# Holding the last activation blocks of a layer on TensorE's queue until the gate products or the prompt's keys are done

## The chip, the cores and the metric

The kernel runs on one core of one Trainium2 chip. The metric is the time of one execution on the device in microseconds. A core has five engines that each work through a queue of their own: TensorE (PE in the profile, its weight loads PEld), VectorE (DVE), ScalarE (ACT), GpSimd (POOL) and SyncE (SP), which here issues the transfers between main memory and the core's own memory. Engines wait for each other only through semaphores.

## The reference, cut to what matters

One step of a two-layer backbone over two streams: a prompt of 128 tokens and a sample of 512 tokens, 1024 wide. Each layer is a mixer (layer 0: retention and a short convolution; layer 1: a gated delta rule and a convolution module) and then an expert mixer in which every token picks 16 of 16,384 experts for each of 8 heads:

```python
def peer_ffn(h, wq, keys, u_tab, v_tab):
    q = (x @ wq).reshape(T, H_P, 2, D_KEY // 2)
    s = jnp.einsum('thpd,hpnd->thpn', q, keys)
    s1, i1 = lax.top_k(s[:, :, 0], TOPK)
    s2, i2 = lax.top_k(s[:, :, 1], TOPK)
    ...
    top_s, sel = lax.top_k(cand_s, TOPK)
    eidx = jnp.take_along_axis(cand_i, sel, axis=-1)
    gates = jax.nn.softmax(top_s)
    ...
        act = jax.nn.gelu(jnp.einsum('td,tkd->tk', xt, u_tab[et]))
        return jnp.einsum('tk,tkd->td', gt * act, v_tab[et])
```

Each layer ends in `xp + ga2p * peer_ffn(hp, ...)` and `xs + ga2s * peer_ffn(hs, ...)`, and layer 1 starts from what layer 0 gives.

## The kernel before, in words

Of the sample's four tiles of 128 tokens, three (384 tokens) are computed densely: all 16,384 experts are multiplied with all tokens, and a matrix of gates, zero for experts that were not picked, selects afterwards. The fourth tile and the prompt gather the rows that they picked (GpSimd issues the gathers, VectorE multiplies and sums the rows). Experts are taken as 128 rows `e` of 128 experts.

`peer_dense` (L1405 on) does the dense part of a layer in two stages.

The first stage has a background: the generator `acts` (L1381) computes for each row `e` a block of activations. A block loads 512 KB of `u` (`ur<-ut`), splits it into a high and a low part (`uh`, a cast on ScalarE; `ul`, a subtraction on VectorE), and runs 24 matmuls of 128x384 (`A<-hHL,uh` and `A<-hHL,ul`, in `peer_act`, L1368); ScalarE applies gelu (`w<-A`, L1379) and the queue of SyncE stores the result to main memory (`wd<-w`). The matmuls of the foreground call `tick` (L165), and a rate decides how many blocks the background has traced by then. The foreground is, in layer 0, the choice of experts and the gates of the sample, and then `mid()` = `odd_p`: the prompt's mixer of layer 1 and the prompt's choice of experts (`peer_start`). In that, 16 pieces of `wq` are projected (`pt<-hT,w`), four times the products with the keys follow (`sc<-keys,q`), `top_keys` (L1160) picks the best on VectorE, and `peer_topk` (lines 1197 to 1238, `top`, `both`, `tv`, `sel`, `eq`, `ef`) finishes the choice there. In layer 1 there is no `mid()`, and the foreground at the stage's end is `gate_matrix` (L1309): three tiles of 8 blocks with 4 groups each, a group being four matmuls `G<-o,o` from one-hot matrices `o` made by VectorE (L1335, L1346) and ScalarE (L1343, L1344). A block of gates is copied (`gst<-G`) and stored (`gd<-gst`).

In the second stage a row `e` loads 512 KB of `v` (`vr<-v`, L1427), its gates (`gt<-gd`, L1433) and its activations (`w<-wd`, L1438). ScalarE casts `vh`, VectorE makes `vl`, multiplies `w<-w,gt` (L1516), ScalarE casts `wh`, VectorE makes `wl`, and 36 matmuls of 128x512 add to `dacc`. Some rows ("fused") have their activation block in this stage. Meanwhile VectorE sums the gathered rows (`row<-row,hn`, `gacc<-row,gel,gacc`, L1274 and L1284).

Each engine runs its instructions in one fixed order. It is set when the kernel is built, by a scheduler that simulates the engines; within `manual_schedule` blocks the named engines keep the order of the code (GpSimd in the first stage, GpSimd, VectorE and ScalarE in the second). `self.mark` is the last gelu: a gather that is issued outside the prompt's lane waits for it (L1248).

Of the kernel before, what the change touches and what calls it, by code (L numbers as in the profile page):

```python
# [2 lines left out]

# [14 lines left out]
P = 128  # L18
# [7 lines left out]
TB = 16  # L26
# [32 lines left out]
SP = (P0, P1)  # L59
MT = 2.4  # L60
GDN_W = 4
PARTS = ((0, 16), (16, 24), (24, 40), (40, 48))
NFIRST = 20

# [19 lines left out]
class Kern:  # L84
    def __init__(self, ctx, tc, A):
        self.tc, self.nc, self.A = tc, tc.nc, A
        e = ctx.enter_context
        self.cp = e(tc.tile_pool(name="consts", bufs=1))
        self.xpool = e(tc.tile_pool(name="x", bufs=1))
        self.rowp = e(tc.tile_pool(name="rowp", bufs=6))  # L90
        self.hpool = e(tc.tile_pool(name="hn", bufs=1))
        self.sm = e(tc.tile_pool(name="sm", bufs=2))
        self.n = 0
        self.bg, self.in_bg = None, False
        self.mods = {}
        self.lane = ""
        self.queue = tc.nc.sync
        self.wt = lambda name: self.pt("w", name)
        self.more, self.turn = None, 0
        self.steps_per_act = self.side_per_act = self.side_rate = self.side_owed = 0.0  # L100
        self.mark = None
        self.side = None

    def nm(self, s):
# [54 lines left out]

    def mm(self, out, lhsT, rhs, start, stop):  # L160

        self.nc.tensor.matmul(out, lhsT, rhs, start=start, stop=stop)  # L162
        self.tick(rhs.free_size() / 600.0)

    def tick(self, us):  # L165

# [933 lines left out]
    def peer_prep(self, st, l, begin=None):  # L1100
# [24 lines left out]
        for jg in range(4):  # L1125
            kt = self.wt("keys")[:, :512]
            self.queue.dma_start(kt, A["keys"][l, jg])
            qs = []
            for j in range(4 * jg, 4 * jg + 4):
                if not late:  # L1130
                    parts(j)
                b = self.proj_split(st, *ws.pop(j)) if st.s else self.proj_t(st, hT, ws.pop(j))
                q = self.a2(st, "q")
                nc.scalar.copy(q[:, :st.T], b[:, :st.T])
                qs.append(q)
                if late:
                    parts(j + 2)
                if pend:
                    self.top_keys(*pend.pop(0))
            for it in range(st.nt):  # L1140
                b = self.bank("sc")
                for j in range(4):
                    self.mm(b[:, j * P:(j + 1) * P], qs[j][:, it * P:(it + 1) * P],
                                     kt[:, j * P:(j + 1) * P], start=True, stop=True)
                t = self.vt("s")
                nc.scalar.copy(t, b)
                if jg == 0:
                    top = (st.scp.tile([P, 512], F32, tag="top", bufs=4, name=self.nm("top")) if st.s
                           else self.vt("top"))
                    st.top[it] = top.rearrange("p (v h c k) -> p v h c k", v=2, h=8, c=2)  # L1150
                pend.append((st, it, jg, t))
                if len(pend) > late:
                    self.top_keys(*pend.pop(0))
# [152 lines left out]
            V.tensor_tensor(acc[half], acc[half], g[half], op=OP.mult)  # L1306
            V.tensor_tensor(st.x[it][:, sl], st.x[it][:, sl], acc[half], op=OP.add)

    def gate_matrix(self, st, tiles, gd):  # L1309

        nc = self.nc
        V, S, PE = nc.vector, nc.scalar, nc.tensor
        for n, it in enumerate(tiles):
            cols = self.gp.tile([P, 4, P], F32, tag="gcols", bufs=1, name=self.nm("gcols"))
            for j in range(2):
# [7 lines left out]
                b = self.bank("gT", (P, P))  # L1323
                self.transpose_to(b, fi)
                V.tensor_copy(cols[:, j, :], b)
            b = self.bank("gT", (P, P))
# [3 lines left out]
            for tb in range(P // TB):  # L1330
                out = self.gp.tile([P, P, TB], F32, tag="gst", bufs=3, name=self.nm("gst"))
                for q in range(TB // 4):
# [4 lines left out]
                    b = self.bank("G", (P, 4, P))  # L1337
                    for j in range(4):
                        t = tb * TB + q * 4 + j
                        o1 = self.gp.tile([P, P], F32, tag="o1", bufs=16, name=self.nm("o1"))  # L1340
                        if j == 3:

                            S.activation(o1, self.iota128, AF.Square, bias=cols[:, 3, t:t + 1])  # L1343
                            S.activation(o1, o1, AF.Relu, scale=-1.0, bias=cols[:, 2, t:t + 1])  # L1344
                        else:
                            V.tensor_scalar(o1, self.iota128, cols[:, 0, t:t + 1], cols[:, 2, t:t + 1],  # L1346
                                            op0=OP.is_equal, op1=OP.mult)
                        self.mm(b[:, j, :], o2[:, j, :], o1, start=True, stop=True)
                    S.copy(out[:, :, q * 4:q * 4 + 4], b.rearrange("p t i -> p i t"))
                nc.sync.dma_start(gd[:, :, n * (P // TB) + tb].rearrange("g p q t -> p g q t"),  # L1350
                                  out.rearrange("p (g q) t -> p g q t", q=GQ))

# [15 lines left out]
    def peer_act(self, st, u, w):  # L1368
# [9 lines left out]
            self.mm(a[:, :N], ul[:, cs], hH[c], start=False, stop=(c == KC - 1))  # L1378
        return self.nc.scalar.activation(w, a[:, :N], AF.Gelu_apprx_tanh)  # L1379

    def acts(self, st, l, es, up, wd, steps):  # L1381

        ur = {i: self.u_load(l, es[i], up) for i in range(2)}
# [2 lines left out]
        for i, e in enumerate(es):  # L1386
# [1 line left out]
                ur[i + 2] = self.u_load(l, es[i + 2], up)  # L1388
            un = self.u_split(i + 1, ur.pop(i + 1), up) if i + 1 < len(es) else None
            w = up.tile([P, wd.shape[2]], F32, tag="w", name=self.nm("w"))  # L1390
            self.mark = self.peer_act(st, u, w)
            self.nc.sync.dma_start(wd[e], w)
            u = un
            due += self.steps_per_act if st.nt - 1 in st.gate else 0
# [10 lines left out]
    def peer_dense(self, st, l, mid=None):  # L1405
# [40 lines left out]
        with self.banks(5), self.tc.tile_pool(name=self.nm("up"), bufs=2, reuse_waits="tile") as up:  # L1446
# [27 lines left out]
            self.rate = RG if mid else RH  # L1474
            self.steps_per_act = STEPS[l]["gates"]
            with self.tc.tile_pool(name=self.nm("gp"), bufs=2, reuse_waits="tile") as self.gp:
                self.gate_matrix(st, tiles, gd)
            if mid:
                for _ in self.side or ():
                    pass  # L1480
# [304 lines left out]
```

## Time and profile before

| | us |
|---|---|
| median of three timed runs | 4157.77 (4157.51 to 4159.66) |
| the profiled execution | 4148.63 |
| its span in the trace | 4146.9 |
| TensorE busy | 3808.5 (92%) |
| VectorE busy | 3393.6 (82%) |
| ScalarE busy | 1510.3 (36%) |

A row of the timeline gives the start in us, the duration in us, the engine, the line, the operation with what it writes and reads, how many instructions it groups, and in brackets how long the engine had idled before it and what ended that. The profile records each of these matmuls twice, so a group of four `G` matmuls is "x8" there, and some records are left out.

### The profile page before, as it was taken

To read this page: it belongs to the slowest core of one execution; us is meant where nothing else is said; L and a number is where in the kernel's file an instruction comes from. 1 tells how busy PE (TensorE), PEld (TensorE's weight loads), DVE (VectorE), ACT (ScalarE), POOL (GpSimd) and SP (SyncE) were. 2 spreads that over 40 slices of the span, in tenths; PEclk is the share of its full clock that TensorE was granted. 3 is DMA by queue.
4 is the path that set the end of the run, shared out by engine and by line. 5 is a ranking of instruction groups with operands and counts; after the bars stand their busy time and mean duration, and the time that the engine had idled before them with its cause. 6 is when DMAs were issued, how large, how long until landed. Compare 5 with 4: busy or idle time off the path is not lost. (4 is left out here: it accounts for less than half of the span.)

```text
span 4146.9 us, 56434 instructions
## 1 busy us (share of the span) xinstructions
PE 3808.5 (92%) x19406; PEld 3124.2 (75%) x19406; DVE 3393.6 (82%) x7171; ACT 1510.3 (36%) x2810; POOL 1457.4 (35%) x1080
## 2 busy tenths in 40 slices
PE   6789879899999998999998998889989989999997
PEld 4453549866899996788884457859989978888886
DVE  5568799997699976988887999569888977788887
ACT  2110123232664542333332364533335733333333
POOL 0106563450024441444435764033011034444442
PEclk9899589999999999999999999899999999999999
DMA  8549698897699888999978977167367899999995
GB/s 291 189 135 358 211 343 292 300 350 251 195 316 361 329 314 301 323 365 359 352 278 328 340 240 250 42 205 278 113 203 234 258 324 325 323 332 333 346 337 186
DMA packets 445776, 1161.99 MB, mean 280 GB/s; under 512 B 39728, under 2 KB 190640, under 8 KB 445232
## 3 DMA queue, kind: packets, MB, share of 16 engines
q1 hardware_dynamic: 290800, 595.23, 40.6%
q0 software_dynamic: 154688, 563.15, 38.4%
q8 instruction: 152, 2.49, 0.2%
q14 instruction: 136, 1.11, 0.1%
HBM read 1062.48 MB, written 95.75 MB: 279 GB/s over the span
## 5 line engine op out<-in xcount | busy, mean ns | idle before, releaser
L1246 POOL DMA_INDIRECT row<-u,eid x512 | 676.7, 1322 | 1318.1 <-ACT w L1379 683.2
L1246 POOL DMA_INDIRECT row<-v,eid x512 | 751.1, 1467 | 1084.4 <-DVE gacc L1284 629.8
L162 PE MATMUL A<-hHL,uh 128*128 128x384 f32 x4096 | 1085.0, 344 | 14.6 <-ACT uh L1355 11.3
L162 PEld LDWEIGHTS A<-hHL,uh 128*128 128x128 f32 x4096 | 748.6, 191 | 46.6 <-issue 20.3
L162 PE MATMUL A<-hHL,ul 128*128 128x384 f32 x2048 | 705.3, 345 | 44.7 <-DVE ul L1356 44.6
L1274 DVE SCALAR_TENSOR_TENSOR row<-row,hn 128x1024 f32<-128x1024 f32 x512 | 614.1, 1218 | 102.0 <-DMA row<-u,eid 91.8
L1284 DVE SCALAR_TENSOR_TENSOR gacc<-row,gel,gacc 128x1024 f32<-128x1024 f32 x508 | 649.8, 1279 | 26.8 <-DMA row<-v,eid 22.1
L162 PE MATMUL dacc<-vh,wh 128*128 128x512 f32 x1536 | 483.5, 396 | 50.2 <-ACT wh L1355 50.2
L162 PE MATMUL dacc<-vl,wh 128*128 128x512 f32 x1536 | 477.9, 392 | 0.0
L162 PE MATMUL pt<-hT,w 128*128 128x128 f32 (+1 forms) x2176 | 455.6, 366 | 23.2 <-DMA w<-wq 12.1
L162 PEld LDWEIGHTS A<-hHL,ul 128*128 128x128 f32 x2048 | 391.4, 191 | 67.5 <-DVE ul L1356 51.0
L162 PEld LDWEIGHTS pt<-hT,w 128*128 128x128 f32 x2176 | 305.2, 196 | 166.7 <-issue 139.8
L1355 ACT CAST uh<-ur 128x1024 fp32r<-128x1024 f32 x256 | 268.1, 1048 | 442.4 <-PE A L162 330.5
L1356 DVE TENSOR_TENSOR ul<-ur,uh 128x1024 fp32r<-128x1024 f32 x256 | 311.7, 1218 | 102.2 <-ACT uh L1355 93.4
L162 PE MATMUL dacc<-vh,wl 128*128 128x512 f32 x1536 | 391.9, 389 | 0.0
L1355 ACT CAST wh<-w 128x384 fp32r<-128x384 f32 (+1 forms) x235 | 137.5, 585 | 659.8 <-DVE w L1516 457.2
L162 PEld LDWEIGHTS dacc<-vh,wh 128*128 128x128 f32 x1536 | 283.4, 189 | 123.8 <-ACT wh L1355 72.6
L1356 DVE TENSOR_TENSOR vl<-vr,vh 128x1024 fp32r<-128x1024 f32 x256 | 312.7, 1221 | 64.8 <-ACT vh L1355 58.2
L162 PEld LDWEIGHTS dacc<-vl,wh 128*128 128x128 f32 x1536 | 291.0, 189 | 62.7
L162 PEld LDWEIGHTS dacc<-vh,wl 128*128 128x128 f32 x1536 | 288.6, 188 | 60.1
L1355 ACT CAST vh<-vr 128x1024 fp32r<-128x1024 f32 x256 | 267.6, 1045 | 54.0 <-PE dacc L162 45.5
L1356 DVE TENSOR_TENSOR wl<-w,wh 128x384 fp32r<-128x384 f32 (+1 forms) x235 | 152.2, 648 | 127.6 <-ACT wh L1355 127.6
(373 smaller groups left out, 5000.3 us busy)
## 6 DMA issues: line engine op xcount, KB each, us to landing
ur<-ut SPq DMA_DIRECT2D x256, 512.0 KB
vr<-v SPq DMA_DIRECT2D x256, 512.0 KB
gd<-gst SPq DMA_DIRECT2D x48, 1024.0 KB
gt<-gd SPq DMA_DIRECT2D x96, 512.0 KB
wd<-w SPq DMA_DIRECT2D x203, 192.0 KB
w<-wd SPq DMA_DIRECT2D x203, 192.0 KB
w<-wq SPq DMA_DIRECT2D x48, 512.0 KB
w<-ada_m SPq DMA_DIRECT2D x48, 512.0 KB
```

Of the source, the lines that this page charges most:

```text
L162: self.nc.tensor.matmul(out, lhsT, rhs, start=start, stop=stop)
L1246: f = self.nc.gpsimd.indirect_dma_start(out=t, out_offset=None, in_=table, in_offset=bass.IndirectOffsetOnAxis(ap=idx, axis=0))
L1274: V.scalar_tensor_tensor(u, u, 1.0, hn, op0=OP.mult, op1=OP.mult, accum_out=act[:, k:k + 1])
L1284: V.scalar_tensor_tensor(gacc, v, t[:, k:k + 1], gacc, op0=OP.mult, op1=OP.add)
L1355: self.nc.scalar.copy(hi, src)
L1356: self.nc.vector.tensor_tensor(lo, src, hi.bitcast(F32), op=OP.subtract)
```

## The change

A table `HOLD` names, for each layer, two marks with a number of blocks: blocks with fewer than that many after them are to come behind the mark. For layer 0 the marks are the prompt's keys, the second product group (`("p", 1, 1)`, 5 blocks) and the last (`("p", 1, 3)`, 3 blocks); for layer 1 the gate blocks 19 (8 blocks) and 23, the last (4 blocks). The products with the keys and the gate products note their last matmul in `self.marks`. Before it issues a held block, `acts` yields until the foreground has traced the mark, and `issue_after` then puts the block's instructions on TensorE behind the mark's on that queue, without a semaphore.

```diff
+HOLD = (((("p", 1, 3), 3), (("p", 1, 1), 5)), ((("G", 1, 23), 4), (("G", 1, 19), 8)))
...
+        self.marks = {}
...
-        self.nc.tensor.matmul(out, lhsT, rhs, start=start, stop=stop)
+        f = self.nc.tensor.matmul(out, lhsT, rhs, start=start, stop=stop)
         self.tick(rhs.free_size() / 600.0)
+        return f
...
+                self.marks[st.name, l, jg] = f.ins
...
+                self.marks["G", l, n * (P // TB) + tb] = f.ins
...
+    def held(self, l, left):
+
+        return next((key for key, n in HOLD[l] if left < n), None)
+
     def acts(self, st, l, es, up, wd, steps):
...
-            self.mark = self.peer_act(st, u, w)
+            key = self.held(l, len(es) - 1 - i)
+            while key and key not in self.marks:
+                yield
+            with self.tc.issue_after(self.marks[key]) if key else nullcontext():
+                self.mark = self.peer_act(st, u, w)
             self.nc.sync.dma_start(wd[e], w)
```

In the built kernel, layer 0 has five held blocks (numbers 123 to 127 of its 128): two stand behind the second products with the keys and three behind the last. Layer 1 has eight: its blocks 67 to 74 of 75, four behind gate block 19 and four behind the last gate product. Lines below the change move by 1 to 13.

On TensorE in layer 0, after the last two products with the keys (`sc`), there stood only products that spread the modulation (`bc`) and then the second stage's `dacc`. Before:

```order
L162 MATMUL sc_13248<-keys_13194,q_13233 128x128
L162 MATMUL sc_13248<-keys_13194,q_13246 128x128
L162 MATMUL bc_13376<-bc_d_13383,ones 128x128
L162 MATMUL bc_13376<-bc_d_13386,ones 128x128
L162 MATMUL bc_13390<-bc_d_13391,ones 128x128
L162 MATMUL bc_13390<-bc_d_13394,ones 128x128
L162 MATMUL bc_13390<-bc_d_13397,ones 128x128
L162 MATMUL bc_13390<-bc_d_13400,ones 128x128
L162 MATMUL dacc_13449<-vh_13455,wh_13460 128x512
```

And now, from the same two products on:

```order
L164 MATMUL sc_13136<-keys_13082,q_13121 128x128
L164 MATMUL sc_13136<-keys_13082,q_13134 128x128
L164 MATMUL A_13232<-hHL_2802,uh_12976 128x384
L164 MATMUL A_13232<-hHL_2810,uh_12976 128x384
L164 MATMUL A_13232<-hHL_2802,ul_12977 128x384
L164 MATMUL A_13232<-hHL_2803,uh_12976 128x384
L164 MATMUL A_13232<-hHL_2811,uh_12976 128x384
```

Three whole blocks, 72 matmuls, now stand between the last key product and the second stage, with the `bc` among and behind them.

On VectorE in layer 0 the choice of the prompt's experts (`sel`, `both`, `eq`, `ef`) is queued together with the second stage's first row (`vl`, `w`, `wl`). Before, the first `vl` stood in the middle of the first search:

```order
L1212 MAX_INDEX sel_13296<-tv_13295,both_13282 128x8 x2
L1211 MAX tv_13295<-both_13282 128x8
L1213 MATCH_REPLACE both_13282<-tv_13295,both_13282 128x50 x2
L1356 TENSOR_TENSOR vl_13456<-vr_13408,vh_13455 128x1024
L1212 MAX_INDEX sel_13296<-tv_13295,both_13282 128x8
L1516 TENSOR_TENSOR w_13414<-w_13414,gt_13410 128x384
L1213 MATCH_REPLACE both_13282<-tv_13295,both_13282 128x50
```

Now, the same `vl` (`vl_13456`) among the last comparisons:

```order
L1228 TENSOR_TENSOR eq_13348<-eq_13348,both_13170 128x800
L282 TENSOR_SCALAR bc_d_21593<-cst,mod_5430 128x128
L1229 TENSOR_REDUCE ef_13227<-eq_13348 128x2x8
L1226 TENSOR_TENSOR eq_13352<-sf_13225,iota_96 128x800
L1361 TENSOR_TENSOR vl_13456<-vr_13408,vh_13455 128x1024
L1529 TENSOR_TENSOR w_13414<-w_13414,gt_13410 128x384
L1228 TENSOR_TENSOR eq_13352<-eq_13352,both_13170 128x800
L1361 TENSOR_TENSOR wl_13461<-w_13414,wh_13460 128x384
```

The first `vl` has moved behind the whole search (`tv`, `sel`) and 10 of the 18 `eq` and `ef` operations; the other eight come between the rows that follow.

On ScalarE in layer 1 the gate copies (`gst<-G`) were followed at once by the second stage's first cast `vh`. Before:

```order
L1344 ACTIVATE o_6175_27956<-o_6175_27956,gcols_27320 128x128
L1349 COPY gst_27892<-G_27895 128x128x4
L1349 COPY gst_27892<-G_27912 128x128x4
L1349 COPY gst_27892<-G_27929 128x128x4
L1349 COPY gst_27892<-G_27946 128x128x4
L1355 CAST vh_28010<-vr_27966 128x1024
```

And now, with `w<-A` the gelu of a held block:

```order
L1353 COPY gst_27721<-G_27775 128x128x4
L1360 CAST uh_27888<-ur_27852 128x1024
L1384 ACTIVATE w_27858<-A_27859 128x384
L1384 ACTIVATE w_27892<-A_27893 128x384
L1360 CAST uh_27923<-ur_27886 128x1024
L1384 ACTIVATE w_27927<-A_27928 128x384
L1384 ACTIVATE w_27955<-A_27956 128x384
L1360 CAST vh_28010<-vr_27832 128x1024
```

The first `vh` now stands behind the gelus of the last held blocks, the very last one included.

## Rows read from the trace of the kernel before

**Rows 1.** Windows: stretch; its length; PE, PEld, DVE, ACT, POOL busy; PEclk; DMA; GB/s.

```profile
1554.30:1591.00 36.70, 36.70 (x174) 29.10 (x173) 23.71 (x41) 11.44 (x24) 13.96 (x14) 1.00 0.89 334
...
1639.70:1652.60 12.90, 2.14 (x13) 1.41 (x11) 12.47 (x84) 3.15 (x6) 0.00 (x0) 0.74 1.00 387
1652.60:1712.70 60.10, 53.96 (x216) 40.98 (x217) 58.85 (x106) 19.36 (x27) 28.42 (x12) 0.97 0.87 305
...
3231.50:3294.00 62.50, 62.17 (x462) 61.85 (x462) 59.88 (x163) 49.53 (x120) 4.30 (x4) 1.00 0.84 250
3294.00:3330.30 36.30, 31.59 (x225) 26.75 (x223) 35.07 (x102) 32.73 (x82) 2.12 (x2) 1.00 0.88 266
```

**Rows 2.** Timeline of PE, from the prompt's projections to the second stage of layer 0.

```profile
1599.65 1.49 PE L162 MATMUL pt<-hT,w 128*128 128x128 f32 x6
...
1619.64 2.05 PE L162 MATMUL pt<-hT,w 128*128 128x128 f32 x16 [0.59 <-DMA w<-wq]
1622.77 5.62 PE L162 MATMUL pt<-hT,w 128*128 128x128 f32 x48 [1.08 <-DMA w<-wq]
...
1639.12 0.61 PE L162 MATMUL sc<-keys,q 128*128 128x128 f32 x4
...
1652.62 1.22 PE L162 MATMUL dacc<-vh,wh 128*128 128x512 f32 x2 [9.88 <-ACT wh L1355]
...
1659.04 0.73 PE L162 MATMUL dacc<-vh,wh 128*128 128x512 f32 x2 [0.43 <-ACT wh L1355]
```

**Rows 3.** Timeline of PE, the thirteenth and fourteenth expert row of that stage.

```profile
1712.76 0.61 PE L162 MATMUL dacc<-vh,wh 128*128 128x512 f32 x2
...
1716.84 0.61 PE L162 MATMUL dacc<-vh,wh 128*128 128x512 f32 x2
```

**Rows 4.** Timeline of DVE, the prompt's choice of experts and the second stage's first rows.

```profile
1640.42 0.86 DVE L1165 MAX8 top<-s 128x8 f32<-128x128 f32 x4
...
1645.61 0.29 DVE L1197 CAST top<-top 128x256 f32<-128x256 uint32 x1
...
1650.15 1.22 DVE L1356 TENSOR_TENSOR vl<-vr,vh 128x1024 fp32r<-128x1024 f32 x1
...
1659.77 1.28 DVE L1284 SCALAR_TENSOR_TENSOR gacc<-row,gel,gacc 128x1024 f32<-128x1024 f32 x1
1660.97 0.82 DVE L1222 TENSOR_TENSOR eq<-sf,iota 128x640 f32<-128x640 f32 x1
...
1675.64 0.99 DVE L1222 TENSOR_TENSOR eq<-sf,iota 128x800 f32<-128x800 f32 x1
```

**Rows 5.** Timeline of PE in layer 1, from the last activations to the second stage.

```profile
3287.22 0.51 PE L162 MATMUL A<-hHL,uh 128*128 128x384 f32 x2
...
3287.74 0.51 PE L162 MATMUL A<-hHL,uh 128*128 128x384 f32 x2
...
3290.16 3.73 PE L162 MATMUL G<-o,o 128*128 128x128 f32 x32
3293.65 0.42 PE L162 MATMUL A<-hHL,ul 128*128 128x384 f32 x1
...
3327.75 1.16 PE L162 MATMUL G<-o,o 128*128 128x128 f32 x8 [0.21 <-DVE o L1335]
3329.12 1.16 PE L162 MATMUL G<-o,o 128*128 128x128 f32 x8 [0.21 <-DVE o L1335]
3343.99 1.22 PE L162 MATMUL dacc<-vh,wh 128*128 128x512 f32 x2 [13.71 <-ACT wh L1355]
```

**Rows 6.** ACT and DVE, a gelu and layer 1's first row of the second stage.

```profile
1588.83 0.49 ACT L1379 ACTIVATE w<-A 128x384 f32<-128x384 f32 x1 [4.53 <-PE A L162]
...
3338.30 1.04 ACT L1355 CAST vh<-vr 128x1024 fp32r<-128x1024 f32 x1 [7.40 <-DMA vr<-v]
...
3342.79 0.56 DVE L1516 TENSOR_TENSOR w<-w,gt 128x384 f32<-128x384 f32 x1 [2.18 <-DMA w<-wd]
```

**Rows 7.** Waits of PE from 3344 to 4122 us: waited in total, times, longest.

```profile
PE dacc L162 <- ACT wh L1355: 34.2, 20, 13.7
```

More of the change, by code (lines that the diff above doesn't have):

```diff
@@ L1 @@
-from contextlib import ExitStack, contextmanager
+from contextlib import ExitStack, contextmanager, nullcontext
 from itertools import chain, islice
@@ L1142, in peer_prep @@
                 for j in range(4):
-                    self.mm(b[:, j * P:(j + 1) * P], qs[j][:, it * P:(it + 1) * P],
+                    f = self.mm(b[:, j * P:(j + 1) * P], qs[j][:, it * P:(it + 1) * P],
                                      kt[:, j * P:(j + 1) * P], start=True, stop=True)
+                self.marks[st.name, l, jg] = f.ins
                 t = self.vt("s")
@@ L1307, in add_out, with gate_matrix @@
             V.tensor_tensor(st.x[it][:, sl], st.x[it][:, sl], acc[half], op=OP.add)
-    def gate_matrix(self, st, tiles, gd):
+    def gate_matrix(self, st, l, tiles, gd):
         nc = self.nc
@@ L1347, in gate_matrix @@
                                             op0=OP.is_equal, op1=OP.mult)
-                        self.mm(b[:, j, :], o2[:, j, :], o1, start=True, stop=True)
+                        f = self.mm(b[:, j, :], o2[:, j, :], o1, start=True, stop=True)
                     S.copy(out[:, :, q * 4:q * 4 + 4], b.rearrange("p t i -> p i t"))
+                self.marks["G", l, n * (P // TB) + tb] = f.ins
                 nc.sync.dma_start(gd[:, :, n * (P // TB) + tb].rearrange("g p q t -> p g q t"),
@@ L1476, in peer_dense @@
             with self.tc.tile_pool(name=self.nm("gp"), bufs=2, reuse_waits="tile") as self.gp:
-                self.gate_matrix(st, tiles, gd)
+                self.gate_matrix(st, l, tiles, gd)
             if mid:
```

## The prediction

> **What bounds the kernel now.** I read the windows first, stretch by stretch, because the 92% of TensorE's busy time is an average. Then came TensorE's timeline at the two places where the held blocks go, VectorE's timeline there, and last what TensorE waits for afterwards.
>
> In layer 0 three stretches follow each other. From 1554.3 to 1591 TensorE has no idle time at all: five activation blocks (123 to 127) and the last projection of the prompt's mixer share it, and VectorE is busy 23.71 of 36.7 us [rows 1]. Then come the prompt's projections from 1599.65, with short waits for pieces of `wq` (0.59 and 1.08 us behind the second keys), and the last key product, which starts at 1639.12 and ends about 1639.7 [rows 2]. Call that end T. From T to the second stage's first `dacc` (1652.62) TensorE stands for 9.88 us, and VectorE is busy 12.47 of 12.9 us [rows 1, 2]. From there to 1712.7 VectorE is busy 58.85 of 60.1 us, so it sets the pace: twelve expert rows take 1712.76 - 1652.62 = 60.14 us, 5.01 each, and the next one takes 4.08 us, which is TensorE's own time for a row [rows 1 to 3]. VectorE is the bound here because the prompt's choice of experts and the dense rows share it.
>
> In layer 1, from 3231.5 to 3294, TensorE (62.17 of 62.5 us) and VectorE (59.88) are both full; then only gate products are left, and TensorE follows VectorE's one-hot matrices (35.07 of 36.3 us busy) with a group every 3329.12 - 3327.75 = 1.37 us [rows 1, 5]. The last gate product ends near 3330.3, and the first `dacc` starts at 3343.99 after 13.71 us of idle time, which is a chain of loads and the splits of the first row [rows 5, 6].
>
> **The change in layer 0.** The five blocks leave the stretch before the prompt's projections. A block is 24 matmuls, and three take 3287.74 - 3287.22 = 0.52 us, so a block is 8 x 0.52 = 4.16 us and five are 20.8 us [rows 5]. The projections start earlier by at most that. What remains of TensorE's work there is 36.7 - 20.8 = 15.9 us, but VectorE keeps 23.71 us less four subtractions `ul` of about 1.2 us, 18.9 us [rows 1, 4], in front of the prompt's last sum, and each step through it (spread, copy, sum) is a round trip that the blocks hid. The stretch cannot be shorter than 18.9 us, which makes 17.8 us the most that the start can move with VectorE in its present order. If TensorE falls to half of its clock while it waits, its 15.9 us become about 32, and the start moves only some 5 us. Between 5 and 17.8 us I take 10, a little nearer to the slow end, because round trips add to VectorE's work.
>
> Two of the blocks (8.3 us) come back among the projections, behind the second keys. There they fill the waits of 0.59 and 1.08 us [rows 2]. T moves by -10 + 8.3 - 1.7 = -3.4 us; with the ends above, by +1.6 to -11.
>
> Behind T stand the other three blocks, 12.5 us on TensorE, beside VectorE's work. They cover the 9.88 us of idle time, and at most 2.6 us stand beyond. The price is the order on VectorE. Before, the first `vl` started 9.73 us after the search's first `MAX8` (1640.42 to 1650.15) [rows 4]. Now it stands behind the whole search and 10 of 18 comparisons. Operations in a row start 0.08 us before the recorded end of the one ahead (1659.77 + 1.28 against 1660.97), so 0.08 is taken off each duration. Worked out from T: 0.7 us to the first `MAX8`; 5.2 us to the cast at 1645.61; 15.4 us from there to the first `eq` (1660.97), less two rows' dense work that stood in it (twice `vl` 1.14, `w` 0.48, `wl` the same, `gacc` 1.2, 6.6 us), 8.8 us; six 640-wide comparisons of 0.74, 4.4 us; four 800-wide of 0.91, 3.6 us; one held `ul`, as large as a `vl`, 1.1 us; and twelve small `bc_d`, by the nearest row of a small tile (the cast's 0.29 us) some 0.2 us each, 2.5 us [rows 4, 6]. That is 26.3 us to `vl`, and 1.2 us for `vl` and 1.2 us from `w` to `dacc` (3342.79 to 3343.99) follow [rows 4 to 6]: 29 us from T, where 12.9 stood before. The three blocks end 12.5 us after T, so about 16 us of idle time follow them.
>
> Some of it comes back, since the search is nearly over by then. Eight comparisons remain, two to a row, so four rows go at 5.01 us and the next eight at 4.08: 52.7 us instead of 60.1. From the thirteenth row on TensorE is the bound in both kernels. The shift there is (29 - 12.9) - (60.1 - 52.7) = +8.7 us behind T, and with T's -3.4 us it is **+5 us**; with the ends of T, -2 to +10. Later TensorE has no slack to return it in, so it is kept.
>
> The Trainium skill ("TensorE: Matmul & The Clock Gate", the table at its head) says that ScalarE's and VectorE's queues are strictly first in, first out, while TensorE can pull weight loads ahead. By that rule the ready `vl` can't pass the search, and the order on VectorE costs what I worked out; the trace agrees so far that the wait of 9.88 us ends by ScalarE's `wh`, behind VectorE [rows 2].
>
> **The change in layer 1.** The eight blocks, 33.3 us, leave the front, where they filled TensorE while VectorE made one-hot matrices. From 3231.5 on, 64 groups are left (512 of the profile's G records to eight for a group). The first 48 go at VectorE's pace: 48 x 1.37 = 65.8 us, plus about 3.5 us for the last tile's columns and one `ul`, which ends near 3301. The last 16 groups and four held blocks need 16 x 0.87 (a group back to back, 3293.65 - 3290.16 = 3.49 us for four) + 16.6 = 30.6 us on TensorE, against 16 x 1.37 + 4 x 1.14 = 26.5 us on VectorE [rows 4, 5]. So the last gate product ends near 3331.5, 1.2 us later than before, although the stretch holds fewer blocks: TensorE then idled while it followed VectorE, and is full only at the end. Behind it four more blocks take 16.6 us, to 3348.
>
> These cover the 13.71 us of idle time and 2.9 us more. But on ScalarE the first `vh` now stands behind the gelu of the very last block, so the first row's splits start when the blocks end: gelu 0.49, `vh` 1.04, `vl` 1.22, then 1.2 us from `w` to `dacc`, 4 us [rows 4, 6]. The first `dacc` comes near 3352 instead of 3343.99: **+8 us**. The transfers for it are issued some 5 us later, behind the store of a held block, and still land before, since the present 13.7 us include them.
>
> Bounds: if the last gate product ends at VectorE's earliest, 3330.3 less the four `ul` behind it, 3325.7, and the row's splits overlap the last block, `dacc` comes at 3342.3; that is -1.7, and with the full clock at its first row, which cost 1659.04 - 1652.62 = 6.42 against 4.08 us in layer 0's first row, -4 [rows 2, 3]. If VectorE's waits pile up, +11. Afterwards TensorE waits 34.2 - 13.7 = 20.5 us in 19 short waits for `wh` [rows 7], set by the order of each row and not by the loads, so a shift stays to the end.
>
> **The sum.** Other instructions move by a few places in the prompt's mixer, where TensorE is full; I count them at nothing, with 2 us to either side. The profiled execution took 4148.63 us, 9 us below the median of 4157.77; the shifts are put on the median: 4157.77 + 5 + 8 = 4171.
>
> **Rivals.**
> - *The shift in layer 0 doesn't pay out, or the two gains cancel:* the prompt's chain moves by up to the 17.8 us that VectorE allows, T by -11, and the thirteenth row by -2; layer 1 is between +1 and +8. This gives 4157 to 4164, no change. For it: VectorE has 13 us of idle time in 36.7 before the projections [rows 1]. Against it: the steps of the mixer's end depend on each other.
> - *Faster, by idle time filled:* both waits, 9.88 + 13.71 = 23.6 us, are filled with blocks that had to run anyway, and the first `dacc` starts at the full clock (PEclk was 0.74 in the stretch of the wait [rows 1]), which saves up to 2.3 us each. If `vl` in layer 0 is not held up by more than the blocks, and layer 1's splits overlap, layer 0 gives -6 to -8 and layer 1 -4: about 4147. For it: TensorE is the bound on both sides of the waits. Against it: VectorE was busy in layer 0's wait, and the orders on VectorE and ScalarE. The Trainium skill (the same page, "Why this matters for your kernels") says to keep TensorE fed without gaps, as its clock drops in them. By that rule this rival gets its 2.3 us twice; the trace agrees that the clock is low around the waits.
> - *Slower by more:* the prompt's chain does not move, because TensorE at its low clock needs as long for 15.9 us of work as it took with the blocks. Then T moves by +6.6 and layer 0 costs 15 us, with layer 1's 8 about 4181. It decides once the chain moves by less than 5 us.
> - *It doesn't do what it says:* only five blocks are held in layer 0, since the others had been traced; if these five were worth nothing either way, only layer 1's +8 would stay, 4166. I count it with "no change".
>
> **How the numbers follow.** What a measurement of this kernel can tell from no change is about 0.2%, 8.3 us. The forecast, slower by 8 to 18 us, has 0.49; slower by more 0.08; no change 0.26; faster 0.17. So faster 0.17, same 0.26, slower 0.57. The forecast's own range is 4166 to 4176. The whole range goes from 4148, inside the faster rival, to 4182.
>
> **What would show it.** Right: the prompt's projections start near 1590; T near 1636; the first `dacc` of layer 0 near T + 29 with some 16 us of idle time behind the held blocks, ended by `wh`; in layer 1 TensorE's waits of 0.21 us grow longer in the stretch of gate products from 3231 on, and `dacc` starts near 3352, 4 us after the last block. Wrong: a first `dacc` of layer 0 directly behind the blocks, projections that start below 1583 or above 1595, or a last gate product in layer 1 well before 3326.

## The result and the profile after

The changed kernel takes 4181.29 us in the median of seven runs (4177.64 to 4190.15), the kernel before 4164.9 us in its seven (4157.51 to 4169.75). The ratio is 1.0054 with a 95% interval of 1.0042 to 1.0066: slower by 0.54%, 22.5 us (17 to 27). The sign was forecast; the forecast of 13 us was too small.

The two profiled executions differ by more, 4190.02 - 4148.63 = 41.4 us, so they can't be subtracted as they stand. The gelu of block 122, the last one ahead of the held blocks, comes 12.0 us later in the trace of after. Of that, 6.2 us stand there at the start of layer 0's first activation block and 7.6 at its gelu, ahead of anything that the change moves. The gelu's two rows on ScalarE, before:

```profile
1555.16 0.50 ACT L1379 ACTIVATE w<-A 128x384 f32<-128x384 f32 x1
```

and after:

```profile
1567.18 0.50 ACT L1384 ACTIVATE w<-A 128x384 f32<-128x384 f32 x1
```

So every stretch is measured from a point inside it. The table gives, in us: A122 to pt, from that gelu to the prompt's first projection; to T, to the end of the last key product; d0, the first `dacc` of layer 0; e12, its thirteenth row; mixer, from layer 0's last `dacc` to layer 1's first activation block; then to the first gate product (G0); Gend, the end of the last gate product; d1, the first `dacc` of layer 1; and the rest of that stage.

| kernel | A122 to pt | A122 to T | T to d0 | A122 to e12 | mixer | to G0 | G0 to Gend | Gend to d1 | d1 to end |
|---|---|---|---|---|---|---|---|---|---|
| before | 44.5 | 84.6 | 12.9 | 157.6 | 581.7 | 381.1 | 181.3 | 13.7 | 779.8 |
| after | 34.0 | 81.1 | 28.7 | 162.9 | 585.5 | 385.4 | 181.7 | 28.0 | 780.4 |
| e1 layer 0 only | 36.1 | 83.6 | 28.7 | 165.3 | 586.1 | 387.1 | 180.6 | 13.7 | 779.2 |
| e2 layer 1 only | 46.4 | 88.7 | 12.9 | 161.6 | 585.6 | 383.3 | 178.8 | 28.4 | 782.2 |
| e3 four w | 35.7 | 82.9 | 28.7 | 164.7 | 586.8 | 384.8 | 179.6 | 32.5 | 780.5 |
| e4 last four | 44.5 | 84.7 | 12.9 | 157.7 | 582.5 | 384.7 | 177.1 | 23.8 | 781.7 |
| e5 four w, stores by ACT | 45.3 | 86.4 | 12.9 | 159.4 | 586.8 | 383.4 | 182.8 | 28.0 | 779.9 |
| e6 last two | 44.5 | 84.7 | 12.9 | 157.7 | 584.4 | 383.5 | 178.7 | 14.8 | 785.8 |
| e7 last two, stores by ACT | 44.5 | 85.2 | 12.9 | 158.2 | 583.0 | 381.0 | 178.5 | 14.5 | 788.2 |
| e8 layer 0, one block | 41.7 | 82.0 | 19.3 | 158.2 | 583.6 | 381.8 | 181.5 | 14.3 | 779.1 |
| e9 no late stores | 45.6 | 87.1 | 12.9 | 160.1 | 586.9 | 386.2 | 179.3 | 21.4 | 783.2 |
| e10 empty table | 44.9 | 85.1 | 12.9 | 158.1 | 587.0 | 385.4 | 181.2 | 13.6 | 779.7 |
| e11 short search | 35.4 | 82.3 | 25.4 | 159.7 | 587.7 | 378.9 | 180.6 | 13.7 | 780.0 |
| e12 one block by ACT | 45.0 | 86.6 | 12.9 | 159.6 | 583.1 | 384.1 | 180.9 | 16.9 | 778.8 |

TensorE's timeline of after in layer 0 answers to [rows 2, 3]:

```profile
1581.66 1.98 PE L164 MATMUL po<-w,cy 128*128 128x512 f32 x4 [2.06 <-DMA w<-od_w_out]
...
1597.55 1.94 PE L437 MATMUL xT<-cst,xn 128*128 128x128 f32 x8 [6.39 <-DVE xn L434]
...
1601.19 2.73 PE L164 MATMUL pt<-hT,w 128*128 128x128 f32 x12
...
1647.67 0.61 PE L164 MATMUL sc<-keys,q 128*128 128x128 f32 x4
...
1676.96 1.22 PE L164 MATMUL dacc<-vh,wh 128*128 128x512 f32 x2 [4.61 <-ACT wh L1360]
...
1730.05 0.61 PE L164 MATMUL dacc<-vh,wh 128*128 128x512 f32 x2
```

Where the blocks had been, TensorE now waits: for the weights of the output projection, and 6.39 us for the prompt's norm. The last wait, 4.61 us, follows a row of `bc` products, not the blocks. VectorE's timeline shows why the `dacc` is so late; it answers to [rows 4]:

```profile
1648.94 0.87 DVE L1169 MAX8 top<-s 128x8 f32<-128x128 f32 x4 [0.78 <-ACT s L1150]
...
1664.38 0.82 DVE L1226 TENSOR_TENSOR eq<-sf,iota 128x640 f32<-128x640 f32 x1
...
1673.72 0.99 DVE L1226 TENSOR_TENSOR eq<-sf,iota 128x800 f32<-128x800 f32 x1
1674.63 1.22 DVE L1361 TENSOR_TENSOR vl<-vr,vh 128x1024 fp32r<-128x1024 f32 x1
1675.77 0.55 DVE L1529 TENSOR_TENSOR w<-w,gt 128x384 f32<-128x384 f32 x1
```

The first `vl` starts 25.7 us after the search's `MAX8` instead of 9.73, although ScalarE had cast its input by 1667.8:

```profile
1666.72 1.04 ACT L1360 CAST vh<-vr 128x1024 fp32r<-128x1024 f32 x1
```

Two windows (columns as in [rows 1]; the blocks behind T, and what follows them) say the same:

```profile
1648.30:1661.20 12.90, 12.90 (x78) 12.90 (x78) 12.19 (x89) 3.22 (x6) 0.00 (x0) 1.00 1.01 388
1661.20:1677.00 15.80, 6.18 (x26) 4.28 (x24) 15.73 (x54) 5.95 (x10) 0.00 (x0) 0.63 0.49 191
```

The blocks do fill 12.9 us of TensorE at its full clock; then VectorE is busy 15.73 of 15.8 us while TensorE has little to do and its granted clock falls to 0.63.

In layer 1 the row on ScalarE that matters is the last block's gelu. Its timeline after:

```profile
3364.50 0.49 ACT L1384 ACTIVATE w<-A 128x384 f32<-128x384 f32 x1 [2.35 <-issue]
...
3368.66 0.49 ACT L1384 ACTIVATE w<-A 128x384 f32<-128x384 f32 x1 [0.61 <-PE A L164]
3380.39 0.49 ACT L1384 ACTIVATE w<-A 128x384 f32<-128x384 f32 x1 [11.24 <-DMA wd<-w]
3380.77 1.04 ACT L1360 CAST vh<-vr 128x1024 fp32r<-128x1024 f32 x1
```

and TensorE's, which answers to [rows 5]:

```profile
3355.71 0.38 PE L164 MATMUL G<-o,o 128*128 128x128 f32 x2
...
3373.11 0.34 PE L164 MATMUL A<-hHL,ul 128*128 128x384 f32 x1
3384.13 1.22 PE L164 MATMUL dacc<-vh,wh 128*128 128x512 f32 x2 [10.68 <-ACT wh L1360]
...
3390.59 0.62 PE L164 MATMUL dacc<-vh,wh 128*128 128x512 f32 x2
```

The block is done at 3373.45, but its gelu starts 6.9 us later, at 3380.39: it writes a `w` buffer, there are two, and the one it needs is still being stored. SyncE's queue shows where that store stood (a row here is an issue; the groups are as in the page):

```profile
3362.17 0.32 SPq L1405 DMA_DIRECT2D wd<-w  x1
3362.59 0.44 SPq L1440 DMA_DIRECT2D vr<-v  x1
3363.08 2.57 SPq L1446 DMA_DIRECT2D gt<-gd  x3
...
3372.61 0.32 SPq L1451 DMA_DIRECT2D w<-wd  x1
3373.92 0.32 SPq L1405 DMA_DIRECT2D wd<-w  x1
```

Between two stores of activations stand eleven loads of the second stage. The gelu of the second of the last four blocks was done by 3365.0, its store was issued at 3373.92 and landed at 3380.28, and the last gelu, which waits for it, starts at 3380.39. `vh` stands behind that gelu. SyncE's waits from 3362 to 3382 us (waited in total, times, longest) say what the store's issue waited for last, the landing of a load:

```profile
SPq L1405 <- DMA gt<-gd: 0.9, 1, 0.9
```

### The profile page after: what moved, and what is told of

Read it like the earlier page. It is cut to its first block, busy times and chain, and to the rows that moved or that the text cites. A ratio compares the mean times of both kernels' runs of the same rounds, so it can differ in the third digit from the quotient of the medians.

```text
span 4188.2 us, 56430 instructions
## 1 busy us (share of the span) xinstructions
PE 3828.0 (91%) x19406; PEld 3136.9 (75%) x19406; DVE 3397.4 (81%) x7171; ACT 1516.0 (36%) x2813; POOL 1450.8 (35%) x1080
## 4 chain that ended last, share of the span: by engine, by line
PE 37%; DVE 14%; issue 9%; DMA 6%; POOL 2%; ACT 2%; DVEq 0%; POOLq 0%; SPq 0%; ACTq 0%
PE dacc L164 19%; PE A L164 9%; DVE row L1278 4%; PE pt L164 3%; POOL row L1250 2%; DMA row<-u,eid 2%; PE po L164 2%; PE G L164 1%; DVE o L1350 1%; DMA vr<-v 1%; DVE cy L514 1%; DVE gacc L1288 1%; DVE vl L1361 1%; DMA row<-v,eid 1%; DVE ul L1361 1%
```

## The experiments

The first four ask which layer the time comes from, and by which mechanism in layer 1.

**e1, layer 0 only.**

```diff
-HOLD = (((("p", 1, 3), 3), (("p", 1, 1), 5)), ((("G", 1, 23), 4), (("G", 1, 19), 8)))
+HOLD = (((("p", 1, 3), 3), (("p", 1, 1), 5)), ())
```

> The table of held blocks is kept for layer 0 and emptied for layer 1. My theory: counted from the last activation block ahead of the hold, layer 0 costs 5 us at the thirteenth expert row (the projections start 10 us earlier, the last key product ends 3.5 us earlier, the first dacc comes 12 us later, and 7 us come back), and what lies between is noise of the execution, so the ratio is near 1.001 (+5 us, 0 to +10), and layer 1's first dacc comes 13.7 us after the last gate product as before. Rival: the five blocks cost the whole 17 us by which the thirteenth row was late in the changed kernel's trace, so 1.004. Second rival: the reordered instructions in layer 1's mixer of the sample cost another 3 to 8 us, seen as a difference that grows between layer 0's last dacc and layer 1's first activation block.

Ratio 1.0025 (1.0013 to 1.0036), 10 us (5 to 15). The thirteenth row is 7.7 us late, the projections start 8.4 us earlier, T to d0 is 28.7 us. Set side by side, after's thirteenth row is 12.0 + (162.9 - 157.6) = 17.3 us later than before's; most of that was a late start of that execution, as my theory had it, and this trace's price is 7.7 us. But the same stretch took 157.6 to 161.6 us in the nine traces without held blocks in layer 0, with before's the shortest, so a trace can't tell 8 from 5. The mixer's 586.1 us is read under e10.

**e2, layer 1 only.** The other half of the table is emptied.

> The table is kept for layer 1 and emptied for layer 0. My theory: the last gate product ends within 2 us of before, counted from the first gate product, and the first dacc comes 28 us after it instead of 13.7 (17 us of blocks and 11 us of a wait of the last gelu for the store that frees its buffer), so +14 to +15 us, ratio 1.0035. Rival: the wait of 11 us was bad luck of one execution, and the first dacc comes 21 us after the last gate product, as forecast: +8 us, 1.002.

Ratio 1.0036 (1.0021 to 1.005), 15 us. The first `dacc` follows the last gate product by 28.4 us, with the last gelu's wait for the store at 11.58 us here, 6.8 of them behind the end of its block: no accident of one execution. The two halves add up, 10 + 15, to the whole's 22.5 within their intervals.

**e3, four buffers `w`** (layer 0 as in the change):

```diff
-            w = up.tile([P, wd.shape[2]], F32, tag="w", name=self.nm("w"))
+            w = up.tile([P, wd.shape[2]], F32, tag="w", bufs=2 + 2 * l, name=self.nm("w"))
```

> The whole change, and in layer 1 the activation blocks have four buffers w instead of two, so that the last gelu waits for no store. My theory: the last gelu follows its block at once, the first vh follows it, and the first dacc comes 4 to 5 us after the last block instead of 10.7: about -6 us against the changed kernel, ratio to before 1.004. Rival: the loads of the first expert row are late as well, since they queue behind the same stores and the transfers are full (about 400 GB/s), so the first dacc moves by less than 2 us and the wait is then at vr or w.

My theory fell: ratio 1.0065 (1.0043 to 1.0087), and Gend to d1 is 32.5 us, not 22. The last gelu now follows its block (done at 3372.02) at once, whatever its bracket names, but a wait in front of the first `vl` takes the place of the old one. ScalarE:

```profile
3372.11 0.49 ACT L1384 ACTIVATE w<-A 128x384 f32<-128x384 f32 x1 [4.71 <-DMA w<-wd]
3372.49 1.04 ACT L1360 CAST vh<-vr 128x1024 fp32r<-128x1024 f32 x1
```

VectorE:

```profile
3384.57 1.22 DVE L1361 TENSOR_TENSOR vl<-vr,vh 128x1024 fp32r<-128x1024 f32 x1 [16.69 <-DMA gt<-gd]
```

`vl` has its input at 3373.5 and starts at 3384.57, behind a transfer. It reads nothing but `vr` and `vh`; what it needs is its place, where buffers of the first stage lay. Of the semaphores that it waits for, the last to be complete is that of a block's store: its gelu was done by 3367.4, it was issued at 3374.80 and landed at 3384.39, 0.18 us before `vl`. The load that the bracket names was issued at 3376.03 and landed only at 3385.64. So a store holds `vl`, issued 7.4 us late and 9.6 us under way. That leaves two readings, stores that stand behind the loads or slow transfers in general, which e5 and e9 were to separate.

**e4, the last four only** (layer 0 none; `HOLD = ((), ((("G", 1, 23), 4),))`).

> Layer 0 holds nothing; in layer 1 only the last four blocks are held, behind the last gate product, and the four before them run in the stretch of the gate products as before the change. My theory: the gate products end 5 us earlier at most (four subtractions of VectorE and four blocks of TensorE leave their stretch, where VectorE sets the pace), then four blocks take 17 us, and the last gelus wait for stores again: the first dacc comes about 26 us after the last gate product, +7 us, ratio 1.002. Rival: holding costs by the count of held blocks (eight cost 14 us, so four cost 7), with the last gate product where it was and the first dacc 21 us behind it. Third: filled idle time pays, and the kernel is faster than before by up to 4 us.

Ratio 1.0018 (1.0004 to 1.0032), 7 us. The gate products end 4.1 us earlier (177.1 instead of 181.3), and d1 follows 23.8 us later. The last two gelus, run together, wait 9.99 us for a store, 3.0 of them behind the end of the last block. So four blocks cost about what was expected of the wait; the count rule gives the same 7 us but not the gate products' gain.

**e5, stores on ScalarE's queue**, with four `w` (layer 0 none):

```diff
-            self.nc.sync.dma_start(wd[e], w)
+            (self.nc.scalar if key and l else self.nc.sync).dma_start(wd[e], w)
```

> Layer 0 holds nothing; layer 1 holds its eight blocks as in the change, their activations have four buffers instead of two, and their stores are issued on ScalarE's queue behind the gelu instead of on SP's, where ten loads stood ahead. My theory: what costs the 11 us beyond the blocks is that buffers (the two of w, and those of the second stage, which lie where the first stage's were) wait for stores that stand behind the loads on SP's queue. Then the last gelu follows its block within 1 us, the first vl no longer waits for a store, and the first dacc comes 5 to 7 us after the last block, 22 to 24 us after the last gate product instead of 28: +8 us, ratio 1.002. Rival: the transfers themselves are the bound (about 5 MB of loads at some 400 GB/s are 12 us, and every one of them is slowed by the others), so the first row's loads land 20 us after their issue wherever the stores are issued, and the ratio stays at 1.0035.

Gend to d1 is 28.0, ratio 1.0027 (1.0015 to 1.0039): nothing won. ScalarE's timeline:

```profile
3364.75 0.49 ACT L1384 ACTIVATE w<-A 128x384 f32<-128x384 f32 x1 [2.67 <-PE A L164]
3367.11 0.33 ACTq L1405 DMA_DIRECT2D wd<-w  x1
...
3374.18 0.33 ACTq L1405 DMA_DIRECT2D wd<-w  x1
3374.61 0.49 ACT L1384 ACTIVATE w<-A 128x384 f32<-128x384 f32 x1 [5.20 <-DMA w<-wd]
3380.31 0.33 ACTq L1405 DMA_DIRECT2D wd<-w  x1
3381.01 1.04 ACT L1360 CAST vh<-vr 128x1024 fp32r<-128x1024 f32 x1 [5.92 <-DMA vr<-v]
```

The stores go out no sooner. Each waits between gelu and issue, the first shown 1.9 us, the third 5.2 us, and stands in ScalarE's own queue now. The second, at 3374.18, costs the last gelu little, since that gelu's block ends only at 3373.94. The third, at 3380.31, holds up `vh`, which otherwise could follow the gelu.

The trace's semaphore records tell why another queue didn't help. The transfers of SyncE and ScalarE take eight semaphores in turn, both queues together, and an issue waits until the transfer that had its semaphore before, eight transfers earlier as a rule, has landed: in e9's trace, the one with every landing on record, none of 1347 issues comes sooner. The three stores are issued 0.07 to 0.08 us behind such landings: of a `ur` load at 3367.04, of the store ahead at 3374.10, and of a `vr` load at 3380.23. So a store stands behind the loads on either queue. The run moves the wait and doesn't tell the readings apart.

**e9, the late stores left out** (layer 0 none). The last four blocks aren't stored; their second-stage rows load row 0's activations instead.

```diff
-            self.nc.sync.dma_start(wd[e], w)
+            if not (l and len(es) - 1 - i < 4):
+                self.nc.sync.dma_start(wd[e], w)
...
-                nc.sync.dma_start(w, wd[e])
+                nc.sync.dma_start(w, wd[0 if l and e in [x for x in range(P) if x not in fused][-4:] else e])
```

> Layer 1 holds its eight blocks as in the change (layer 0 none); left out are the stores of the last four blocks' activations, whose second-stage rows load another row's activations instead, so the loads are as many as before. Theory A (store behind the loads): no gelu and no buffer of the second stage waits for a late store, so the last gelu follows its block within 1 us, and the first dacc comes 22 to 24 us after the last gate product instead of 28. Theory B (the transfers are the bound): 0.75 MB less of about 5 MB at 400 GB/s is 2 us less at most, so the first dacc comes 26 to 28 us after the last gate product, and the wait is for vr or gt.

Theory A: Gend to d1 is 21.4 us, at the same count of loads. The last gelu runs at once and `vh` behind it; ScalarE, then TensorE:

```profile
3355.82 0.49 ACT L1384 ACTIVATE w<-A 128x384 f32<-128x384 f32 x1 [4.58 <-PE A L164]
3356.20 1.04 ACT L1360 CAST vh<-vr 128x1024 fp32r<-128x1024 f32 x1
```

```profile
3359.56 0.73 PE L164 MATMUL dacc<-vh,wh 128*128 128x512 f32 x2 [3.84 <-ACT wh L1360]
```

3.84 us from the last block to `dacc`, where the forecast had 4. The run to set beside it is e2, with the same blocks and the stores kept: the late stores cost 28.4 - 21.4 = 7.0 us there, as much as the last gelu's 6.9 us in after.

The whole kernel still took 1.0035 (1.0020 to 1.0050) of before, as e2 did: what d1 won didn't show in the time. Part of it is lost again in the stage behind (783.2 us, 782.2 in e2, 779.8 before), where the first fused row waits for its `u`, as in e7. From the first gate product to the end of the stage, which takes 973.5 to 974.9 us in the five traces without held blocks in layer 1, e9's trace takes 983.9 us and e2's 989.4: 5.4 of the 7.0 us stay won. Intervals of 8 to 21 us (e9) and 9 to 21 us (e2) over before can neither show nor exclude that.

**e6 and e7, two blocks in layer 1** behind the last gate product, with stores on SP's queue and on ScalarE's. `HOLD = ((), ((("G", 1, 23), 2),))`.

> Layer 0 holds nothing; in layer 1 two blocks are held behind the last gate product, their stores on SP's queue as in the change. My theory: the gate products end 2 us earlier, the two blocks take 8.3 us inside the idle 13.7, and no gelu waits for a buffer, as there are two; but the second store stands behind the first rows' loads, and the first vl waits for it, so the first dacc comes about 18 us after the last gate product instead of 13.7: +2 us. Rival: idle time is filled and nothing waits, -2 us.

> As the run with two blocks held behind the last gate product of layer 1, but the two stores are issued on ScalarE's queue. My theory: they land before the first row's loads, so the first dacc comes 14 us after a last gate product that is 2 us earlier: -2 us, ratio 0.9995. Rival (loads are the bound): the same as on SP's queue.

Ratios 1.0015 (1.0004 to 1.0026) and 1.0009 (0.9997 to 1.0022). In both, d1 comes 1.5 to 2 us earlier counted from G0, e6 against my expectation; and in both the stage behind it gives back 6 to 8 us, which I had not expected. In e6 the wait for the second store, which I had put before the first `vl`, comes one row later: the second row's `vh` starts 0.07 us after that store, issued at 3346.97, has landed. ScalarE, then TensorE:

```profile
3356.37 1.04 ACT L1360 CAST vh<-vr 128x1024 fp32r<-128x1024 f32 x1 [7.69 <-DMA wd<-w]
```

```profile
3359.74 1.09 PE L164 MATMUL dacc<-vh,wh 128*128 128x512 f32 x2 [4.62 <-ACT wh L1360]
```

In e7 there is no such wait, but another. TensorE:

```profile
3348.81 1.22 PE L164 MATMUL dacc<-vh,wh 128*128 128x512 f32 x2 [6.22 <-ACT wh L1360]
...
3368.67 1.01 PE L164 MATMUL A<-hHL,uh 128*128 128x384 f32 x2 [4.61 <-ACT uh L1360]
```

The first fused row's block waits 4.61 us for `u`. Before, the loads of `u` for the first two fused rows stood ahead of the second stage's first loads; now their buffers are still the held blocks', and they stand behind. Filled idle time is paid back 11 us later in e6 and 20 us later in e7.

**e12, one block, its store by ScalarE.** `HOLD = ((), ((("G", 1, 23), 1),))` with e5's second line.

> Layer 0 holds nothing; in layer 1 one block is held behind the last gate product, its store issued on ScalarE's queue, so that nothing new stands on SP's queue ahead of the first loads. My theory: the idle 13.7 us there are the landing of the first expert row's loads, which a block on TensorE can't shorten; the gate products end 1 us earlier (one subtraction less on VectorE), the first dacc follows 13.5 to 14.5 us later, and the load of u for the first fused row, one place later on SP's queue, costs up to 2 us behind it: ratio 0.9995 to 1.0005. Rival: a block of 4.2 us put into idle time is 4 us gained, ratio 0.999, with the first dacc 4 us earlier counted from the first gate product.

Ratio 0.9998 (0.9986 to 1.0010): no change, as expected, but not by the expected steps. The first `dacc` comes 16.9 us after the last gate product, not 13.5 to 14.5, so TensorE still waits 12.69 us behind the block. What comes late is VectorE's product of the first row (before: [rows 6], 2.18 us):

```profile
3360.86 0.56 DVE L1529 TENSOR_TENSOR w<-w,gt 128x384 f32<-128x384 f32 x1 [5.26 <-DMA w<-wd]
```

The load that it waits for is issued 6.8 us behind the last gate product in both kernels, but lands 8.8 us after its issue instead of 5.6. (SP's queue also waits 3.0 us for the block's store, ahead of its third `vr`.) A block in idle time gained nothing here.

**e8, one block in layer 0.** `HOLD = (((("p", 1, 3), 1),), ())`.

> Layer 1 holds nothing; in layer 0 one block is held, behind the last keys, and VectorE's order is that of before (the first vl in the middle of the search). My theory: layer 0's price is the place of the first vl behind the search, and not the blocks behind the keys: here the projections start 2 to 4 us earlier, the one block (4.2 us) lies in the idle 9.9 us, and the first dacc and the thirteenth row come 2 to 4 us earlier, ratio 0.9993. Rival: any block behind the last keys delays the second stage, whose buffers lie where the first stage's were: the first dacc comes later by 3 us or more against the last key product, ratio 1.000 or above.

Ratio 1.0001 (0.9991 to 1.0012). My expectation was wrong in a premise: VectorE's order is not that of before. Its timeline:

```profile
1657.27 0.82 DVE L1226 TENSOR_TENSOR eq<-sf,iota 128x640 f32<-128x640 f32 x1
1658.01 1.22 DVE L1361 TENSOR_TENSOR vl<-vr,vh 128x1024 fp32r<-128x1024 f32 x1
```

The first `vl` stands behind the whole search and one comparison, T to d0 is 19.3 us, and what T gained is gone. The rival's number was right, its reason (buffers) was not: `vl` starts without a gap behind that comparison.

**e11, a shorter search** (layer 0 as in the change, layer 1 none). 15 of the prompt's 18 comparisons in layer 1 are left out.

```diff
...
+        if st.name == "p" and self.mark is not None:
+            V.memset(ef, 0.0)
+            groups = groups[:1]
+        for k, n, hs in groups:
```

> Layer 0 holds its five blocks (layer 1 none); of the prompt's choice of experts in layer 1, 15 of the 18 comparisons are left out (their rows' numbers are zero), so ahead of the first vl on VectorE there are 3 of them instead of 10, some 5.9 us less, and one small memset more. My theory (the first dacc of layer 0 waits for VectorE's search): it comes 22 to 23.5 us after the last key product instead of 28.7. Rival (it waits for the buffers of the second stage, which the held blocks free, or for loads): it stays within 1.5 us of 28.7.

There is one execution of this kernel, so only its trace is read. T to d0 is 25.4 us: between the two. The search is shorter by what was left out, but other small operations are queued ahead of `vl` and now wait for TensorE. VectorE:

```profile
1677.20 0.71 DVE L282 TENSOR_SCALAR bc_d<-cst,mod 128x128 f32<-128x128 f32 x2 [0.56 <-PE bc L164]
1678.43 0.71 DVE L282 TENSOR_SCALAR bc_d<-cst,mod 128x128 f32<-128x128 f32 x2 [0.52 <-PE bc L164]
1679.61 0.72 DVE L282 TENSOR_SCALAR bc_d<-cst,mod 128x128 f32<-128x128 f32 x2 [0.47 <-PE bc L164]
1680.24 1.22 DVE L1365 TENSOR_TENSOR vl<-vr,vh 128x1024 fp32r<-128x1024 f32 x1
```

The last comparison's result was converted at 1676.42; the ping-pong of `bc_d` and `bc` then takes until 1680.24. Neither buffers nor loads hold `vl` (it starts as soon as its queue lets it), but the gain is 3.3 us and not 5.3 to 6.7.

**e10, the empty table.** `HOLD = ((), ())`.

> The changed kernel's code with an empty table, which gives every engine the order of before. The ratio is 1.000. Its trace tells how much the stretches that the change does not touch differ between executions: from layer 0's last dacc to layer 1's first activation block (581.7 us before, 582.5 to 586.8 in six other traces) and from there to the first gate product (381.1 before, 381.0 to 387.1). My theory: both are scatter of the transfers, and this trace lies inside these bounds, above the one of before. Rival: the held blocks of layer 0 cost 4 us in the mixer, and this trace gives 581 to 583.

Ratio 1.0005 (0.9992 to 1.0019), and the mixer takes 587.0 us with nothing held, more than in the changed kernel (585.5). So the mixer's 4 us and the 4 us up to G0 are no more than the scatter between executions, and the trace of before was at the low end of both. That held blocks in layer 0 cost nothing there isn't shown: the kernels with them have another order on VectorE in that mixer, and take 585.5 to 587.7 us.

## Why the forecast was right in sign and too small

- **Layer 0, the chain ahead of the keys: right.** Forecast -10 us for the projections; measured -10.5 in after, -8.4 in e1, -8.8 in e3. T moved by -3.5, -1.0 and -1.6, forecast -3.4; A122 to T itself scatters from 84.6 to 88.7 us in the nine traces without held blocks there, so no single one of these confirms the forecast. The weights' loads (2.06 us and two more waits near 1.8) are a part that I had not named; I had only round trips through VectorE and the clock.
- **Layer 0, the place of the first `vl`: right.** Forecast 29 us from T to `dacc`, measured 28.7 in all three traces that hold the five blocks. The trace of after shows VectorE busy without a gap of note from 1648.94 to `vl`, and e8 shows the same with another length. The thirteenth row came 5.3, 7.7 and 7.1 us late, counted from the shortest of those nine traces; forecast 5, which lies at the edge of what e1's time allows (5 to 15 us).
- **Layer 1, the gate products: near, in after by luck.** Forecast +1.2 us for the last gate product, measured +0.5 (181.7 against 181.3), but -2.5 to +1.6 in the five traces with the same eight blocks. Eight blocks fewer ahead of them give little gain, since TensorE is busy without a gap from 3326 to the last gate product. As a sign I had named longer waits of TensorE among these products; they stayed at 0.21 us and became more.
- **Layer 1, from the last block to `dacc`: this step failed.** I wrote that "the first row's splits start when the blocks end" and gave 4 us. Measured: 10.7, of which 6.9 are the last gelu's wait behind the end of its block. The chain of 4 us itself was right, as e9 shows (3.84), but the gelu has to wait for a buffer whose store has not landed. I had named the store of one held block on SP's queue as a delay of the loads; I did not ask the reverse, which store stands behind the loads, and who waits for that. The term "+8" was 12 to 15 us in the traces of the eight blocks with two `w` (Gend to d1 28.0 to 28.4, together with the gate products' change). In the trace of after, layer 0's 5.3 us and layer 1's 14.8 make 20.1 of the 22.5 us, and these 6.9 are most of the 9 us that the forecast lacked.
- **The bounds of layer 1** went to +11, and 14.8 lies outside. **The base:** the shifts were put on the median of three runs of before, 4157.77; seven runs give 4164.9. So 7 of the 10 us between 4171 and 4181.29 are the base and not the change.
- **The rivals.** "Faster, by idle time filled" fell: e7 and e12 fill idle time with one or two blocks, the first `vr` issued as soon behind the last gate product as before (1.2 us), and get nothing. "No change, the two gains cancel" fell for the whole change. "Slower by more" named a chain in layer 0 that doesn't move; it moved, and the extra time was in layer 1; its 4181 meets the measured 4181.29 only because the base lay 7 us higher. That only five blocks are held in layer 0 is true, but they are not worth nothing: e1 is slower by 5 to 15 us.
- **The clock.** The first row behind the wait cost 3390.59 - 3384.13 = 6.46 us, no better than the 6.42 in layer 0 of before and hardly better than the 6.61 of layer 1's first row before; the 2.3 us that the faster rival counted on were not won. The rule of the Trainium skill that stood beside this rival ("TensorE: Matmul & The Clock Gate", "Why this matters for your kernels": no idle gaps, since the clock drops in them) agrees with the rows on the clock, 0.63 in the window behind the blocks; on the time it didn't decide, as e7 and e12 filled part of the gap for nothing.

What stays open: the sum of the traces' shifts, 5 to 8 in layer 0 and 12 to 15 in layer 1, agrees with 22.5 us within its interval. That late stores delay the first `dacc` is shown by e9 and by the landings in after, e3 and e6; that the whole kernel loses 5 to 7 us by them is read from single traces, and the times of e2 and e9 don't resolve it. Whether the other order in layer 1's mixer, a term that I had put at nothing, costs a few us isn't shown either.

## What to carry to other kernels

Before work is moved into an engine's idle time, list what that work still has to hand back: buffers it occupies, stores it owes, and the loads that need its buffers. Read on the issuing queue what those stores will stand behind, and check whether another queue shares its semaphores, since then it doesn't free them. And when an order is made by a scheduler, read the new order of the engine that was busy during the idle time: a block that fits on TensorE can still push the next stage's first operation behind everything that VectorE has queued.

## What the runs showed that was not expected

- Stretches with the same order differ between executions: the mixer took 581.7 to 587.0 us in nine traces without held blocks in layer 0, and the stretch behind it 381.0 to 386.2 in the same nine, while the dense stretch of layer 0 behind the thirteenth row (e12 to the last `dacc`) took 473.4 us in every trace. The stretch in which TensorE is the bound repeats to 0.01 us, the two others don't.
- A store issued on ScalarE's queue held that engine's next instruction: in e5 `vh` stood for 5.2 us behind a store that could not be issued until a load had landed.
